# Zeros written early to the head of each output row, from a second ring, in a kernel that turns images by 180 degrees

## Chip, cores, metric

One core of one Trainium2 chip. The metric is the device time of one execution in microseconds, as the median of several runs. All times compared below are of fast runs, or of single runs (then said so) beside runs of the kernel before on the same chip; the granted clock was 1.000 in every run.

## The reference

```python
x = np.random.randn(32, 3, 256, 256).astype(np.float32)      # 25.17 MB in, 25.17 MB out
np.rot90(x, k=2, axes=(-2, -1))                               # each 256x256 plane read backwards
```

Flattened, each of the 96 planes is simply reversed. There is no arithmetic: the kernel loads, reverses and stores.

## The kernel before

The 96 planes are cut into 3 groups of 32. A plane is 4 rows of 16,384 float32 (64 KB), so a group fills 128 partitions of SBUF with one 64 KB row each. VectorE reverses inside a row; the store writes the four rows of a plane in reversed order.

```python
    x4 = x...("(g n) (s e) -> g (n s) e", n=32, s=4)      # cut
    o4 = out...("(g n) (s e) -> g n s e", n=32, s=4)      # cut
    A, Bt, Ct = three tiles [128, 16384]; T = one tile [128, 2048]     # cut
    def load(t, g, lo=0, hi=E):
        nc.sync.dma_start(out=t[:, lo:hi], in_=x4[g][:, lo:hi])
    def store(t, g):
        nc.sync.dma_start(out=o4[g][:, ::-1, :], in_=t[:, :])
    # across(dst, src): 4 copies of 4096 columns, backwards; inside(t): 12 copies of 2048, by way of T
    load(A, 0, 0, N)        # N = 512 columns: 2 KB of each row
    load(A, 0, N, E)
    load(Bt, 1)
    across(Ct, A)
    store(Ct, 0)
    load(A, 2)
    inside(Bt)
    store(Bt, 1)
    across(Ct, A)
    store(Ct, 2)
```

## Time and profile before

| | before |
|---|---|
| time, median of 3 (later 4) runs | 122.99 us (123.06) |
| span in the profile | 121.2 us |
| DMA share of the span | 97.4% |
| VectorE busy | 27% |

The lines that carry the reading stand in the prediction. What else is used below are the landings: the issues of the kernel before, with engine, number, size and the time from issue to landing in us.

```profile
A<-in_x_dram SPq DMA_DIRECT2D x1, 7936.0 KB, 21.4
Bt<-in_x_dram SPq DMA_DIRECT2D x1, 41.4
```

Both loads are queued one behind the other at the start. So a change in the first number shows what happened up to the end of A, and a change in the second what happened up to the end of Bt. I use the trace's records of single DMA packets (start, duration, size, queue). "Too long" below always means: the mean over the 16 engines of how much a row's packet took over 2.342 us (62 KB row of A) or 2.418 us (64 KB row), the durations of nearly all such rows; sums over 8 KB or 2 KB packets are taken over 0.309 and 0.084 us each, and given per engine. A "ring" is the queue of transfers that one issuing sequencer (SP or ACT) feeds.

### The profile page before, as it was taken

The numbers are of one execution on the slowest core, as the hardware profiler recorded it, in microseconds if no ns is written. First come the engines' busy times: TensorE is split into PE (matmuls) and PEld (weight loads), VectorE is DVE, ScalarE is ACT, GpSimd is POOL, SyncE is SP. The second block draws the span as 40 slices with busy tenths as digits, with TensorE's granted clock in tenths as the row PEclk, the third lists the DMA queues.
The fourth block names the chain that finished last, engine by engine and source line by source line (L and its number), as shares of the span: only waits on it lengthen the run. The fifth ranks groups of instructions, "written<-read, shape, count | busy, mean of one in ns | idle before, by whom it ended". The sixth has DMA issues, their size and how long they took to land.

```text
span 121.2 us, 75 instructions
## 1 busy us (share of the span) xinstructions
DVE 32.5 (27%) x20; POOL 0.2 (0%) x4
## 2 busy tenths in 40 slices
DVE  0000000599400079999100000009990000000000
POOL 0000000000000000000000000000000000000000
DMA  9977987997899497799789977997798779877980
GB/s 336 421 335 335 650 356 335 433 606 346 346 454 584 173 519 346 346 519 519 346 346 627 411 346 346 649 389 346 346 649 389 346 346 649 389 346 346 649 389 0
DMA packets 1008, 50.33 MB, mean 415 GB/s; under 512 B 112, under 2 KB 112, under 8 KB 240
## 3 DMA queue, kind: packets, MB, share of 16 engines
q1 hardware_dynamic: 1008, 50.33, 97.4%
HBM read 25.17 MB, written 25.17 MB: 415 GB/s over the span
## 4 chain that ended last, share of the span: by engine, by line
DMA 58%; DVE 13%; DVEq 2%; SPq 1%; issue 0%
DMA A<-in_x_dram 58%; DVE Ct L55 13%; DVEq L109 2%; SPq L61 1%; SPq L58 0%; DVEq L55 0%
## 5 line engine op out<-in xcount | busy, mean ns | idle before, releaser
L55 DVE COPY Ct<-A 128x4096 f32<-128x4096 f32 x8 | 17.8, 2290 | 46.3 <-DMA A<-in_x_dram 46.3
L55 DVE COPY T<-Bt 128x2048 f32<-128x2048 f32 x4 | 4.9, 1227 | 11.6 <-DMA Bt<-in_x_dram 11.5
L55 DVE COPY Bt<-T 128x2048 f32<-128x2048 f32 x4 | 4.9, 1227 | 0.1
L55 DVE COPY Bt<-Bt 128x2048 f32<-128x2048 f32 x4 | 4.9, 1226 | 0.1
L98 POOL MEMSET const-bfloat16-1.0<- 128x1 bf16 x1 | 0.1, 102 | 0.0
L98 POOL MEMSET const-uint8-127<- 128x1 uint8 x1 | 0.1, 102 | 0.0
L98 POOL MEMSET const-float32-1.0<- 128x1 f32 x1 | 0.1, 99 | 0.0
L98 POOL MEMSET const-float32-0.0<- 128x1 f32 x1 | 0.1, 98 | 0.2 <-issue 0.2
## 6 DMA issues: line engine op xcount, KB each, us to landing
A<-in_x_dram SPq DMA_DIRECT2D x1, 7936.0 KB, 21.4
A<-in_x_dram SPq DMA_DIRECT2D x1, 256.0 KB, 2.8
out_dram<-Ct SPq DMA_DIRECT2D x2, 30.4
Bt<-in_x_dram SPq DMA_DIRECT2D x1, 41.4
A<-in_x_dram SPq DMA_DIRECT2D x1, 49.4
out_dram<-Bt SPq DMA_DIRECT2D x1, 43.0
```

The source lines that it names most:

```text
L55: tc.keep_in_program_order(nc.vector.tensor_copy(out=dst, in_=src))
L61: nc.sync.dma_start(out=o4[g][:, ::-1, :], in_=t[:, :])
L98: nc = _bacc.Bacc("TRN2", target_bir_lowering=False, num_devices=1)
L109: with _tile.TileContext(nc) as tc:
```

## The change

The idea is to write a little to the output early, in the same pattern as the first store, on a ring of its own, so that whatever the first write pays is paid before it matters. The true store overwrites the zeros.

```diff
+    Z = 128
...
+    zeros = Ct[:, 0:Z]
+    nc.vector.memset(zeros, 0.0)
     load(A, 0, 0, N)
     load(A, 0, N, E)
+    nc.scalar.dma_start(out=o4[0][:, ::-1, 0:Z], in_=zeros)
     load(Bt, 1)
```

## The prediction

> **What bounds the kernel now.** I read the page's summary first, then the waits, the chain with the issues, and last the DMA rate in stretches of one packet time.
>
> ```profile
> span 121.2 us, 75 instructions
> DVE 32.5 (27%) x20; POOL 0.2 (0%) x4
> DMA  9977987997899497799789977997798779877980
> GB/s 336 421 335 335 650 356 335 433 606 346 346 454 584 173 519 346 346 519 519 346 346 627 411 346 346 649 389 346 346 649 389 346 346 649 389 346 346 649 389 0
> DMA packets 1008, 50.33 MB, mean 415 GB/s; under 512 B 112, under 2 KB 112, under 8 KB 240
> q1 hardware_dynamic: 1008, 50.33, 97.4%
> ```
>
> The 16 DMA engines are full (97.4% of the span, on one queue) and VectorE works 27% of it, so the span is set by bytes over DMA rate. The packet line gives the packet's size: 112 are tiny (7 transfers x 16 engines, one completion each), 128 more are the 2 KB rows of the small first load, and the other 768 are whole rows of 62 or 64 KB. So one row is one packet, 8 rows of each group per engine, 48 long packets per engine. In the records of single packets a 65,536 B row takes 2.418 us as a median, load or store, one right behind the other: 16 x 65,536 B / 2.418 us = 433.7 GB/s. 48 x 2.418 = 116.1 us is therefore the floor of the data; the other 5.1 us of the span are start, end and stalls. A slice of 3.03 us holds one to two packet ends per engine, so 346 and 649 in the slices are only beats between the two periods. But 173 occurs once: a hole near 39.4 to 42.4 us.
>
> ```profile
> DVE Ct L55 <- DMA A<-in_x_dram: 46.3, 2, 23.7
> DVE T L55 <- DMA Bt<-in_x_dram: 11.5, 1, 11.5
> SPq L61 <- DVE Ct L55: 61.5, 2, 32.0
> ```
>
> ```profile
> 1.17 21.43 DMA A<-in_x_dram
> 22.63 8.91 DVE Ct L55 x4
> 32.31 49.42 DMA A<-in_x_dram
> ```
>
> VectorE waits for loads; the sequencer that issues the stores waits for VectorE, but this does not starve the DMA: the first store is issued at 31.56 us and its engines are still on the load of Bt until about 42 us. So what VectorE does is off the path, with some 9 us to spare at the first store.
>
> Where the non-data time lies follows from the landings. A has landed at 1.17 + 21.43 = 22.60 us; Bt at 43.01 us (VectorE starts on it then); the second A at 32.31 + 49.42 = 81.73 us. Between Bt and the second A lie 16 packets per engine: 38.72 us, or 2.420 each, no loss. Between A and Bt lie 8: 20.41 us where 8 x 2.418 = 19.34, a loss of 1.07 us. The narrow stretches find it:
>
> ```profile
> 33.80:36.22 2.42, 0.00 (x0) 0.00 (x0) 1.00 1.00 433
> 36.22:38.64 2.42, 0.00 (x0) 0.00 (x0) 1.00 1.04 433
> 38.64:41.06 2.42, 0.00 (x0) 0.00 (x0) 1.00 1.36 406
> 41.06:43.48 2.42, 0.47 (x1) 0.00 (x0) 1.00 1.00 433
> ```
>
> The last two columns are the DMA share (over 1 because a packet counts where it ends) and GB/s. In one round the 16 packets took 3.28 to 4.00 us instead of 2.42 (median 3.52, so +1.10). It is the last row of Bt, directly before the first row of the first store. At the second change from load to store (about 81.5 us) and at the change back every packet is within 0.25 us of the 2.418. So it is a cost paid once by each engine, when it meets its first store: I call it the first-write stall. The start shows a similar thing for reads: among the 2 KB packets (median 0.084 us) an engine's first ones take up to 0.71 us, and the first 62 KB row takes a median 2.62 against 2.34 us later. The small load ahead of A looks like the same idea for the read side.
>
> **What the Trainium skill says.** "DMA: Bandwidth & Descriptors", Specifications, gives a fabric ceiling of 435 GB/s; the 433.7 above agrees, so the rows cannot get faster and only the stalls are to be had. The same page, "Issuing engines are not separate DMA queues": transfers issued from ACT and SP run on the same 16 DMA engines and interleave, which saves only issue time. The kernel before uses one queue, so its trace doesn't test this; if it holds, the zeros take DMA time from the loads. "Queues, rings and completion order" there: an engine round-robins between its rings packet by packet, a packet being typically 9 to 17 descriptors. This trace disagrees on the size, as the 1008 packets are one row each; so the zeros should be 8 packets of 512 B per engine, taking turns with the loads. "Back-pressure in remote DMA" says for transfers between cores that stalled writes also stall the source engine's other queues; whether local stores behave so no run here shows yet, and it decides most of the sum.
>
> **The change part by part.** Nothing is removed from the program; the instruction order of every engine is kept.
> 1. A memset of 128 columns on VectorE. The copies give 1227 ns for 2048 columns and 2290 for 4096, so 0.52 ns a column and 0.16 us fixed: 0.16 + 0.07, about 0.23 us, at a time when VectorE idles until 22.6 us. On the path: 0.
> 2. One more issue, on ACT, which did nothing. SP's issue at 0.73 us had its first packet at 1.73 us; ACT waits for the memset, so I expect its issue near 1.0 and its first packet at 2.0 to 2.4 us, among the small packets of A. On the path: 0.
> 3. 128 packets of 512 B, 65.5 KB, 8 per engine. From 63,488 to 65,536 B a packet grows by 76 ns, and a 2 KB packet takes 84: so 8 ns fixed and 19 ns for 512 B, 27 ns each and 0.22 us per engine. Doubled for changing ring and direction that is 0.4. I put +0.3 us on the path, since the engines have no gap later in which to take it back.
> 4. The first store meets a warm path: -1.06 us if the stall belongs to the engine's first write to the output. That Bt's store and the third group's store show none, on rows never written before, speaks for one payment each. I give this 0.8: -0.85 in the mean.
> 5. The stall itself is paid by the zeros at the start. If it holds up the loads on the same engine, +1.06 comes back in full. If it runs beside the stalls of the first reads (which I put at about 1.2 us: 22.60 - 1.73 to the first packet - 19.34 of data = 1.53, less about 0.3 from last packet to landing), most is hidden. I know of nothing that decides it and take half: +0.5.
> 6. New waits: the first copy into Ct waits for the zeros to have been read and landed, and the first store waits for them too (it overwrites them). In the worst turn-taking, one 512 B packet per 62 KB row, the zeros end with A at about 22.6 us, so the copy moves by at most one packet, 2.4 us, against 9 us to spare. On the path: 0.
> Sum: -0.85 + 0.3 + 0.5 = -0.05 in the mean. The single most likely outcome, cured and partly hidden, is -1.06 + 0.3 + 0.4 = -0.36, so I put the point a little to that side: 122.99 - 0.29 = 122.7 us.
>
> **The rivals.**
> - Cured and hidden entirely: -1.06 + 0.22 gives 122.15. For it: the first reads stall at the same moment, and the changed kernel has been aimed at just this. Against: the loads share the engine with the zeros.
> - Cured but paid in full: -1.06 + 1.06 + 0.3 gives 123.3, the stall only moved. For it: in the kernel before the stall did stretch a load packet that preceded the store, so it does block other work on its engine.
> - Not cured, because the stall belongs to the ring of SP or is forgotten in the 34 us up to the first store: 123.3, or up to 124.3 if the start stalls as well. Against: later stores, 20 us of loads after the first, find the path warm.
> - The wait of the copy for the zeros becomes the bound. It would take more than 9 us of delay, which no turn-taking gives.
>
> **Range and chances.** The cases run from 122.15 to 124.3, with the last reached only if both halves fail. The range 122.0 to 123.6 holds all but the corner and some tenths for how the engines spread. 2% is 2.46 us: faster than 120.5 would need more than the whole stall (1.06) and the whole read stall (1.2) to vanish together, slower than 125.4 needs more than both costs in full. So: faster 0.01, within 2% 0.97, slower 0.02.
>
> **What would show it.** Step 4: the slice with 173 GB/s is gone, and from A's landing to Bt's there are 19.4 us instead of 20.4. Step 5: A lands later than 22.60, by 0.3 if the stall is hidden and by 1.4 if paid in full. Step 3: 144 more packets, under a second queue of far under 1%. Step 6: the first copy still begins with A's landing, and the first store is issued 9 us before it can start. Wrong would be a hole that stays with the second queue idle by then, or a time outside the range: then the stall is not one of first writes, or two queues disturb each other in the steady part.

## The result, and the profile after

123.31 us median of 4 runs (123.08 to 123.51), against 123.06 (122.95 to 123.18) before: ratio 1.002, 95% interval 0.9998 to 1.0041. A ratio compares the fast runs of both kernels of the same rounds, so it is not quite the ratio of the medians quoted. The same within 2%, and if anything slower; the range 122.0 to 123.6 holds it.

The summary of the kernel after, in the order of the lines shown for before:

```profile
span 121.6 us, 79 instructions
DVE 32.7 (27%) x21; POOL 0.2 (0%) x4
DMA  8977987997799597798779877977798779879980
GB/s 294 463 337 337 653 358 337 391 647 345 345 410 625 237 453 345 345 647 388 345 345 647 388 345 345 690 345 345 345 647 388 345 345 647 388 345 431 561 388 0
DMA packets 1152, 50.40 MB, mean 414 GB/s; under 512 B 128, under 2 KB 256, under 8 KB 384
q1 hardware_dynamic: 1008, 50.33, 97.0%
q10 hardware_dynamic: 144, 0.07, 0.2%
```

A second queue has come with 144 packets (128 of zeros, 16 completions), 0.2% of the DMA time. The hole in the rate is still there: 237 GB/s in the same slice that had 173, the only value below 290 apart from the last slice. The landings have not moved either (21.4 and 41.4 before):

```profile
A<-in_x_dram SPq DMA_DIRECT2D x1, 7936.0 KB, 21.5
Bt<-in_x_dram SPq DMA_DIRECT2D x1, 41.5
```

Now the stretches of one packet time around it, in the kernel after (the last two columns are DMA share and GB/s):

```profile
34.06:36.48 2.42, 0.00 (x0) 0.00 (x0) 1.00 1.00 433
36.48:38.90 2.42, 0.00 (x0) 0.00 (x0) 1.00 1.18 460
38.90:41.32 2.42, 0.00 (x0) 0.00 (x0) 1.00 1.09 325
41.32:43.74 2.42, 0.55 (x1) 0.00 (x0) 1.00 1.00 433
```

A packet is counted whole in the stretch in which it starts. The share above 1 is spread over two stretches here, because they cut the packets at another place; together they hold 0.27 x 2.42 = 0.65 us of excess, and the second has a rate of 325. The packet records say it more exactly: the last row of Bt is 1.105 us too long, against 1.133 before. Nothing was cured.

The waits and the chain of the kernel after:

```profile
DVE Ct L59 <- DMA out_dram<-Ct: 24.0, 1, 24.0
DVE Ct L59 <- DMA A<-in_x_dram: 23.9, 1, 23.9
```

```profile
1.02 23.93 DMA out_dram<-Ct
24.95 0.04 DVEq L59
...
25.04 8.91 DVE Ct L59 x4
...
34.69 47.42 DMA A<-in_x_dram
```

The zeros (issued by ACT at 1.02 us) land only at 24.95 us, and the first copy waits for them until 25.04, where before it began at 22.63. This wait has entered the chain of what ended last, but it costs nothing: the store is issued 2.4 us later, at 33.96 us, and its engines are on Bt until over 42 us. That the chain passes a wait doesn't prove that the wait sets the time.

Where did the small loss come from? Each zero packet took exactly 0.027 us, 8 per engine: 0.216 us. The last row of the kernel ends at 119.45 to 119.96 us before and at 119.66 to 120.44 after: the earliest engine is 0.21 later, which is the zeros; the latest 0.48, as the engines have also drifted somewhat further apart (0.78 us against 0.51). In the mean over the engines the last row ends 0.19 us later.

### The profile page after: what moved, and what is told of

It reads as the page before. It is cut to its first block, busy times and chain, and to the rows that moved or that the text cites. A ratio compares the mean times of both kernels' runs of the same rounds, so it can differ in the third digit from the quotient of the medians.

```text
span 121.6 us, 79 instructions
## 1 busy us (share of the span) xinstructions
DVE 32.7 (27%) x21; POOL 0.2 (0%) x4
## 2 busy tenths in 40 slices
DMA packets 1152, 50.40 MB, mean 414 GB/s; under 512 B 128, under 2 KB 256, under 8 KB 384
## 4 chain that ended last, share of the span: by engine, by line
DMA 59%; DVE 13%; DVEq 2%; SPq 1%; issue 0%
DMA A<-in_x_dram 39%; DMA out_dram<-Ct 20%; DVE Ct L59 13%; DVEq L116 2%; SPq L65 1%; DVE Ct L79 0%; DVEq L59 0%; SPq L62 0%
## 6 DMA issues: line engine op xcount, KB each, us to landing
out_dram<-Ct ACTq DMA_DIRECT2D x1, 64.0 KB, 23.9
```

## Experiments

Two questions: are the zeros' bytes the whole cost, and what is the stall, if not the first write to the output? The edits "No zeros", "More packets", "Nothing queued" and "A dummy store of whole rows" are made to the kernel before, the others to the changed kernel.

**The changed kernel once more** (no edit, 5 rounds).

> The changed kernel once more. Theory 'only the bytes' (the zeros cost their 8 packets of 0.027 us per engine and cure nothing): 0.2 to 0.35 us slower than the kernel before, ratio 1.002 to 1.003, and the last row before the first store again about 1.1 us too long. Rival 'noise': ratio 1.000 to 1.001, or a stall that is gone in another look.

Measured: 123.23 us (123.16 to 123.51, 6 runs) against 123.12 (11 runs), ratio 1.0014, interval 1.0001 to 1.0027. Bt's last row 1.043 us too long. The ratio is 0.17 us, in keeping with 0.216 us of bytes; noise alone is just outside the interval. In this look the zeros landed at 23.02 us instead of 24.95, and its run took 123.16 us against 123.38; both lie in the spread of this kernel's runs, so this look says nothing for or against the wait.

**Four times the zeros** (3 rounds).

```diff
-    Z = 128
+    Z = 512
```

> The changed kernel with Z = 512: 2 KB of each row. Theory 'only the bytes': 8 packets of 0.084 us, so 0.67 us over the kernel before: 123.75, ratio 1.0055, and Bt's last row still 0.9 to 1.1 us too long. Rival 'turns cost more than bytes' (each of the 8 turns also upsets the load beside it, as the 8 KB run hints with its 1 us above the bytes): 0.9 us or more over the kernel before, ratio above 1.007.

Measured: 123.60 against 122.91 us, ratio 1.0059 (1.0042 to 1.0076), so 0.7 us: the 0.67 us of the bytes. The zero packets took 0.084 us each; Bt's last row stays 1.100 too long. The bytes explain the loss at both sizes.

**No zeros: ACT writes the true 512 B, late** (5 rounds).

```diff
-    across(Ct, A)
-    store(Ct, 0)
+    copy(Ct[:, 0:K], back(A, E - K, E))
+    nc.scalar.dma_start(out=o4[0][:, ::-1, 0:Z], in_=Ct[:, 0:Z])
+    (the other three copies)
+    nc.sync.dma_start(out=o4[0][:, ::-1, Z:E], in_=Ct[:, Z:E])
```

> No zeros: ACT's ring writes the true first 512 B of each output row at about 25 us, after the first copy, and SP's store leaves these columns out. Theory 'forgotten' (a write 15 us ahead warms what a write 35 us ahead doesn't): stall ahead of the first long store under 0.3 us, time 122.0 to 122.4. Theories 'the ring' and 'long writes only': stall stays 1.1 us, time 123.0 to 123.2, as no byte is added.

Measured: 123.09 against 123.12 us, ratio 0.9999 (0.9987 to 1.0011); the small packets ran from 28.98 us on, 8 per engine taking turns with the rows of Bt and of the store, and Bt's last row was 1.077 too long. So "forgotten in 34 us" falls. With no byte added, the second ring and its turns cost nothing that could be measured.

**The zeros on SP's own ring** (5 rounds).

```diff
     load(A, 0, 0, N)
+    nc.sync.dma_start(out=o4[0][:, ::-1, 0:Z], in_=zeros)
     load(A, 0, N, E)
-    nc.scalar.dma_start(out=o4[0][:, ::-1, 0:Z], in_=zeros)
```

> The zeros issued on SP's ring, between the small and the large load of A. Theory 'the ring' (the stall belongs to the first store on SP's own ring): the stall ahead of the first store is gone, A lands later by up to 1.1 us, time between 122.3 (stall hidden at the start) and 123.4 (only moved). Theory 'not the first write' (size of the write, or time passed since, decides): the stall of 1.1 us stays ahead of the first store, time 123.3 to 123.6, with the first load issued late costing nothing or up to 0.3.

Measured: 125.47 against 123.12 us, ratio 1.0186 (1.016 to 1.0212): 2.35 us slower, well clear of noise, which neither theory had. The stall stayed: 1.072 on Bt's last row, so being on SP's ring is not enough to pay it. The loss is at the start. The timeline of this kernel (start, length):

```profile
0.73 0.38 SPq L62 DMA_DIRECT2D A<-in_x_dram  x1
1.17 0.62 SPq L81 DMA_DIRECT2D out_dram<-Ct  x1
1.82 0.58 SPq L62 DMA_DIRECT2D A<-in_x_dram  x1
```

The long load of A is issued at 1.82 us instead of 1.17. Its first rows start 0.63 us later in the mean over the engines (the 0.22 us of zeros run in that gap) and are 0.73 us too long instead of 0.23, so they end 1.13 later. The last rows end 1.10 later in the mean: that is the whole loss of the average engine. The rest goes with engines out of step: the last rows end between 120.39 and 122.98 us, 2.59 apart, and the span ends with the last, 3.02 us later than before. Why they part is open.

**More packets ahead of the first store** (single look; a first try of it, with a group that does not exist, didn't build).

```diff
     load(Bt, 1)
+    nc.sync.dma_start(out=T[:, :], in_=x4[2][:, 0:J])      # 8 KB rows, not used
```

> The kernel before with one more load behind Bt (8 rows of 8 KB per engine, some 2.4 us), so that 9 more packets stand ahead of the first store on SP's ring. Theory 'ahead of the first store': Bt's last row takes 2.42 us again and the last 8 KB packet, about 0.31 us otherwise, takes 1.1 us longer. Rival 'a place in the ring or a moment in time': the stall stays on Bt's last row, at 38.5 to 42.7 us. Time about 125.5 either way.

Measured: 125.26 us beside 123.11. The landings of this kernel:

```profile
T<-in_x_dram SPq DMA_DIRECT2D x1, 1024.0 KB, 43.3
Bt<-in_x_dram SPq DMA_DIRECT2D x1, 40.3
```

Bt now lands in 40.3 us and not 41.4: its last row is 0.001 us too long. The 8 KB packets behind it are too long by 0.97 us in all (mostly on the third to the seventh sixteen of the 128 in order of start, where I had expected it on the last). So the stall goes with what follows, the first store, and neither with a place in the ring nor with a moment.

**Nothing queued behind the first store** (3 rounds): the second load of A made to wait until Bt is turned.

```diff
-    load(A, 2)
     inside(Bt)
+    tc.keep_in_program_order(nc.vector.memset(A[:, 0:1], 0.0))
+    load(A, 2)
     store(Bt, 1)
```

> The kernel before with the second load of A issued only after Bt is turned (near 58 us, by a one-column memset of A that it must wait for), so that nothing is queued behind the first store when it starts. Theory 'first long write': the stall of 1.1 us stays on the last row of Bt; time 122.9 to 123.3. Rival 'depth of the queue' (the load queued behind the store causes it): stall gone, time 121.9 to 122.2.

Measured: 123.05 against 123.11 us, ratio 0.9991 (0.9977 to 1.0006), Bt's last row 1.193 too long. The queue's depth is not the cause.

**A dummy store of whole rows** (single look).

```diff
+    nc.vector.memset(Ct[:, :], 0.0)
     load(A, 0, 0, N)
     load(A, 0, N, E)
+    store(Ct, 0)
     load(Bt, 1)
```

> The kernel before with a whole dummy store of zeros (64 KB rows) to the first group between the loads of A and Bt, overwritten later. Theory 'first long write': the last row of A takes 1.1 us too long, ahead of the dummy, and Bt's last row, ahead of the true store, takes 2.42. Rival 'each first long store behind loads issued together, or the place in time': stalls on both, or only on Bt's. Time 142.4 to 143.5 (8 x 2.418 = 19.3 more, plus 1.1 if it stalls twice).

Measured: 143.16 us beside 123.11. The landing of A in this kernel:

```profile
A<-in_x_dram SPq DMA_DIRECT2D x1, 7936.0 KB, 22.5
```

22.5 instead of 21.4: the stall is now ahead of the dummy, 0.974 us on A's last row. Ahead of the true store, to the same addresses, only 0.215 is left on Bt's last row. So a long earlier transfer does pay for most of it, where 512 B per row did not.

**8 KB of zeros, taking turns** (ACT, single look) **and in a row** (SP, single look).

```diff
-    Z = 128
+    Z = 2048                       # first kernel; the zeros stay on ACT
-    nc.scalar.dma_start(...zeros)
+    nc.sync.dma_start(...zeros)    # second kernel only: behind the load of A, ahead of Bt
```

> The changed kernel with Z = 2048: 8 KB of each row instead of 512 B, 8 packets of about 0.31 us per engine, 2.4 us more in all. Theory 'long writes only': an 8 KB write is long enough to pay, so the stall shows beside one of the first zero packets (over 0.31 us or a stretched load row before it) and Bt's last row takes 2.42; time 125.4 to 125.6 as the stall moves. Rival 'any earlier write from another ring is useless': Bt's last row keeps its 1.1 us; time 125.4 to 125.7. The packet records decide, not the time.

> 8 KB of zeros per row, but on SP's ring between the loads of A and Bt, so that the 8 packets of an engine (64 KB) run in a row instead of taking turns with loads. Theory 'bytes written in a row': the last row of A ahead of them takes 0.8 us or more too long and Bt's last row at most 0.3, as with the dummy of whole rows. Theory 'length of the single write': 0.3 to 0.4 at the zeros and 0.6 to 0.8 on Bt's last row, as when they took turns. Time near 125.5 (2.47 more of data) in both.

Measured, taking turns: 126.72 us beside 123.11; Bt's last row still 0.727 too long, the rows of A 0.584 in sum against 0.272 in the kernel before. Each zero packet took 0.309. In a row: 127.17 beside 122.91; A's last row 1.185 too long, Bt's 0.026. The landing of A in the second:

```profile
A<-in_x_dram SPq DMA_DIRECT2D x1, 7936.0 KB, 23.0
```

The same 64 KB per engine in the same 8 KB writes pay the whole stall when they run in a row, and about a third when a load row stands between each two. So the length of the single write isn't what counts. But the two kernels also differ in the ring, and no run has the turns on SP or the row on ACT, so the share of each is not separated. Both also lost more than the 2.47 us of bytes (3.6 and 4.3 us). In the mean over the engines the last row ends 2.41 and 2.59 us later than in the kernel before, so about the bytes; the rest is the engines' ends, 2.0 and 2.3 us apart.

**The same rows, written inside SBUF** (single look).

```diff
-    Z = 128
+    Z = 2048
-    nc.scalar.dma_start(out=o4[0][:, ::-1, 0:Z], in_=zeros)
+    nc.sync.dma_start(out=T[:, :], in_=zeros)
```

> The same 8 KB rows at the same place of SP's ring, but written to T inside SBUF and not to the output. Theory 'the read from SBUF is what is first': the stall shows ahead of this copy and no more than 0.3 us is left on Bt's last row. Theory 'the write to HBM is what is first': Bt's last row keeps 1.0 to 1.1 us and A's last row shows none. Time near 125.5 in both.

Measured: 125.52 us beside 122.91, so 2.6 for 2.47 of bytes. The stretches of one packet time at the end of A (first two lines) and at the end of Bt (last three) in this kernel:

```profile
17.60:19.94 2.34, 0.00 (x0) 0.00 (x0) 1.00 1.46 434
19.94:22.60 2.66, 0.00 (x0) 0.00 (x0) 1.00 0.08 24
...
38.70:41.12 2.42, 0.00 (x0) 0.00 (x0) 1.00 1.00 433
41.12:43.54 2.42, 0.00 (x0) 0.00 (x0) 1.00 1.00 433
43.54:45.96 2.42, 0.41 (x1) 0.00 (x0) 1.00 1.00 433
```

15 of the 16 last rows of A start in the first stretch and are counted whole there, with a share of 1.46; the sixteenth is the only packet that starts in the second, 24 GB/s: A's last row is 1.147 us too long. At the end of Bt, ahead of the first write to the output of the whole program, the rate is 433 without a break, 0.000 too long. So the stall is not one of writing to HBM at all. In the kernels that begin with loads it comes when an engine first moves a run of bytes out of SBUF, wherever they go.

**The same copy as the very first transfer** (single look): memset, copy to T, then the loads, held in this order on SP.

```diff
-    load(A, 0, 0, N)
-    load(A, 0, N, E)
-    nc.scalar.dma_start(out=o4[0][:, ::-1, 0:Z], in_=zeros)      # Z = 2048
+    (kept in program order, all on SP:)
+    nc.sync.dma_start(out=T[:, :], in_=zeros)
+    the loads of A (two) and Bt as before
```

> The copy inside SBUF (8 KB rows, from Ct to T) as the very first transfer, before any load; it waits for its memset of about 1.8 us, so the loads start some 4.8 us later (about 2.3 us of waiting and 2.5 us of copying). Theory 'first read of SBUF by an engine, whatever came before': some of the 8 KB packets or what follows at once lasts 1.1 us too long and Bt's last row takes 2.42: time 126.6 to 127.8. Theory 'first change from HBM reads to SBUF reads': no stall at the copy, as no read of HBM came before it, and Bt's last row 1.1 us too long: about 127.7.

Measured: 128.99 us beside 122.97, above both ranges. The 8 KB packets are 1.07 us too long in sum, A's first row 0.46 (before: 0.23), Bt's last row 0.27. A change from reading HBM to reading SBUF is thus not needed, as then Bt's last row would have kept its 1.1. But how much of the 1.07 is this stall and how much the start of the very first transfer (0.34 us on the 2 KB packets of the kernel before, none on them here) this run doesn't separate. Of the 1.07, 0.83 lies on the last 48 of the 128 packets in order of start, right ahead of the first load, and 0.24 on the 80 before them. So a rival stands: that the stall comes with the first change between the two sources, SBUF and HBM, in either direction. In all other kernels the two readings say the same. This run does show that doing it first hides nothing: the start became longer, not fuller.

**2 KB per row in a row** (SP, single look): as the second of the 8 KB kernels, with Z = 512.

> 2 KB of zeros per row on SP's ring between the loads of A and Bt: 8 packets in a row, 16 KB per engine, instead of taking turns as in the run with 2 KB from ACT (which left Bt's last row 1.1 us too long). Theory 'bytes in a row, 16 KB is enough': A's last row 1.0 to 1.2 us too long, Bt's last row under 0.3. Theory 'in proportion to the bytes up to 64 KB': 0.2 to 0.4 on A's last row and 0.7 to 0.9 on Bt's. Time 123.5 to 123.8 in both.

Measured: 124.41 us beside 122.97 (a single run too), above the range, with the engines' ends 1.5 us apart. A's last row 0.243 too long, Bt's 0.709. The stall is paid in parts.

What was paid early and what was left, in us per engine, one look each:

| early bytes out of SBUF, per engine | way | too long there | left on Bt's last row |
|---|---|---|---|
| none (before) | | | 1.133 |
| 4 KB (after; again) | turns | none seen | 1.105; 1.043 |
| 4 KB | in a row, at the start | up to 0.5 (A's first row) | 1.072 |
| 16 KB | turns | none clear | 1.100 |
| 16 KB | in a row | 0.243 | 0.709 |
| 64 KB | turns | about 0.3 | 0.727 |
| 64 KB | in a row | 1.185 | 0.026 |
| 64 KB | in a row, inside SBUF | 1.147 | 0.000 |
| 64 KB | in a row, inside SBUF, before any load | 1.07, the start included | 0.269 |
| 512 KB | in a row (whole rows) | 0.974 | 0.215 |

The "turns" are all on ACT's ring, the rows all on SP's. The copy inside SBUF pays 1.15 us, and 16 KB in a row pays 0.95 in its two parts. More is not always paid in full: 512 KB left 0.215. Where next to nothing was paid early, the looks lie between 1.04 and 1.19, so differences under 0.15 say little. No version was faster than the kernel before: every way of paying early costs the bytes and gives back at most what it paid.

## Why the prediction was right, and which of its steps failed

The range and the class were right; the point (122.7) was 0.6 us low, and the outcome came from the rival "not cured: 123.3", for which step 4 had left a chance of 0.2. As for the mechanism the range held by luck: it was drawn wide enough to hold the case in which the main step fails, and the time of 123.3 was also that of "cured but paid in full", so it could not tell the two apart. The prediction's own sign of being wrong is what did: the hole stayed, long after the second queue's only transfer had landed (24.95 us).

- **What bounds the kernel**: held. The DMA engines were 97.0% busy after; the copies moved by 2.4 us, and the time did not follow.
- **Step 3, the bytes**: 0.027 us a packet and 0.22 per engine were predicted from the growth of packets with size; 0.027 and 0.216 measured. The allowance of up to 0.4 for changing ring and direction was not needed: true data split over two rings cost nothing (ratio 0.9999).
- **The reading of the stretches**: a packet does not count "where it ends" but whole where it starts. In the kernel before, 15 of the 16 last rows of Bt start between 38.64 and 41.06 us and end only after 42.1; counted there, they give 406 GB/s and a share of 1.36. The slice with 173 is one in which only 8 rows start. The stall does not hang on this, as the packet durations show it.
- **Step 4, "the first store meets a warm path: -1.06 us", chance 0.8**: this is what failed. I read the stall as an engine's first write to the output. All the evidence I had (once per engine, at the first store, not at later stores to new rows) fits just as well with the first run of bytes taken out of SBUF, which I did not consider. The copy inside SBUF (a single look) decides between the two: it takes the stall over in full. And the zeros are too few to pay: 4 KB per engine left 1.04 to 1.11 of it, as against 0.026 behind 64 KB in a row.
- **Step 5, "the stall itself is paid by the zeros at the start"**: did not come about either. A's rows were too long by 0.256 us in sum after and 0.272 before. Steps 4 and 5 failed together, so -0.85 + 0.5 became 0, and the sum became step 3 alone.
- **Step 2**: ACT issued at 1.02 us as estimated, but the first zero packet came at 5.16 us and not at 2.0 to 2.4: SP's small packets and first long row went ahead, and from then on one zero packet followed each long row.
- **Step 6**: the delay of the copy was 2.4 us, as the worst case allowed, and cost nothing. That the first copy would still begin with A's landing was wrong. The estimate of the memset, 0.23 us, was 0.165.

What stays open is the mechanism. Shown is: once per engine, about 1.1 us, tied in kernels that begin with loads to the first run of bytes out of SBUF, not to the output, the moment or the queue's depth, and not cured by merely using SP's ring; paid in parts by runs in a row on SP's ring, less by the same bytes taking turns from ACT's. Not separated are the turns from the ring, and the first run out of SBUF from the first change between the two sources. What inside the engine fills or settles in that time no run shows. Nor is it shown why the engines end 1.5 to 2.6 us apart in the kernels with early writes in a row and with 8 KB in turns, and 2.0 where the copy inside SBUF comes first, but only 0.64 where it follows the load of A.

## What to carry to other kernels

Before warming up "the first write", find out what is first about it: a dummy with the same source and another destination costs one run, and here it overturned the reading. A warm-up on engines that were already full could here only move the cost, and added its own bytes; it could pay only where the engines would stand idle, which no run here tried. And a new wait in the chain of what ended last is not yet a loss: look whether what it delays had to queue anyway.

## What the Trainium skill lacked or had wrong

- No page that I read has the stall at an engine's first run of bytes out of SBUF: 1.04 to 1.19 us on the last row ahead of it where next to nothing was paid early, moved whole by a copy inside SBUF (1.147 there, 0.000 left). It would belong to "DMA: Bandwidth & Descriptors".
- The same page, "Queues, rings and completion order", puts a packet at typically 9 to 17 descriptors. Here each row was a packet of its own, 512 B to 64 KB (1152 packets = 8 transfers x (128 rows + 16 completions)). Its rule that an engine takes turns between its rings packet by packet held: 8 zero packets among the long rows, from 5.16 to 22.29 us. With packets this long, 4 KB per engine on the second ring took 22.0 to 23.9 us from issue to landing.
